# Row tiles at other distances from the weights, a two-tile copy, 128-row broadcasts and a wide norm in a float32r network kernel

## The chip, the cores and the metric

One core of a Trainium2 chip runs the whole program in one launch. The metric is the device time of an execution in microseconds (us), lower is better; the kernel before was timed three times. All instruction times come from one profiled execution of that kernel. The engines are PE (TensorE matmul), DVE (VectorE), ACT (ScalarE), POOL (GpSimd) and SP (SyncE, which issues the weight DMAs).

## The reference, cut

256 tokens of width 1024 go through one recurrent block, two hybrid attention layers and a last norm, all in float32.

```python
def first_block(x, ...):                     # DEPTH 1
    hn = rmsnorm(h, norm1_w)
    gates, z, xbc, dt_raw, lru_x, lru_y = split(hn @ w_in)
    ...                                      # Mamba-2 mixer, RG-LRU mixer, gated sum
    h = h + merged @ w_out
    hn = rmsnorm(h, norm2_w)
    g, u = split(hn @ w_ffn_in)              # 2816 wide each
    h = h + (silu(g) * u) @ w_ffn_out
    return rmsnorm(h, norm_f_w)

def hybrid_layer(x, ...):                    # twice
    proj = rms_norm(x, attn_norm_w) @ w_in
    ...                                      # retention, sparse and dilated attention
    x = x + mixed @ w_out
    h = rms_norm(x, mlp_norm_w)
    return x + square(relu(h @ w_up)) @ w_down   # 4096 wide
```

## The kernel before, in words

Activations lie with the feature on the partition and the 256 tokens (`T`) along the row, as row tiles of 128 features by 256 tokens. Every large product is made of float32r matmuls in three parts: `mm3` (L330 to L333) multiplies the high part of the weight with the high part of the row tile, the high with the low, and the low with the high. In `run_a` (L335) a 128x128 block of the weight is loaded and a 128x256 row tile streams past it; in `run_b` (L361) a block of the row tile is loaded and up to 512 columns of the weight stream. A unit is a 512-column strip of a weight matrix; it is cut into pieces of 128x1024 elements, 24 matmuls in `run_a`. The weights come over SP's queue as 1 MB chunks into three `raw` buffers. ACT makes the high part of a piece (`hi`, L254), DVE the low (`lo`, L255), into rings of five; `next_piece` splits four pieces ahead of use. The order of units is a list (`PLAN`); small work (scans, attention, transposes) is inserted between matmuls by generators, moved on by `tick` after each pair of column blocks (counts in `TICKS` and `YIELDS`).

The stages in order of time are: `in` (input projection with both mixers between), `wo`, the FFN's input (`fg`, `fu`, tiles `xnh`/`xnl`, 44 pieces) and output (`fo`, tiles `ah`/`al`), then per layer `l` the mixer's projections (`mix`, `run_a` and `run_b`), its output (`mx` tiles), the MLP's `up` (`xnh`/`xnl`, 32 pieces) and `down` (`dn`, tiles `mah`/`mal`; layer 0 as `run_a`, layer 1 as `run_b`).

`pair_tiles` (L407) allocates the high and low tiles of a stage with some padding and starts the data at an element offset from the table `OFF`; everything else is allocated in steps of 512 bytes. With the address of the moving tile less that of the loaded weight, modulo 512 bytes, as the **distance**, each stage therefore has one distance, the same for all its row tiles, `hi` and `lo` alike.

`Norm` (L886) collects the squares of the residual: `add` accumulates them into a 128x2x256 tile `sqa` (L910), `bank_done` also makes the row tiles and, at the last one, a small square root `pre` (L923) that brings ACT's table. The row tiles are not scaled by the norm; the scale `rb` multiplies the matmul's result when the PSUM banks are evacuated. `hook` runs `sums` after a given piece of the first unit and `spread` after another (marks `FM`, `QM`, `UM`): `sums` (L946) reduces `sqa` over the partitions by fp32 matmuls with a column of ones (two passes each), eight passes per accumulator; `rsqrt_act` or `rsqrt_cols` work on 128x2; `spread` (L481, L484) turns the two columns into a 128x256 tile `rb` with two transposes and a copy by ACT.

`bc` (L668) belongs to the Mamba mixer. For two heads it broadcasts a row of cumulative sums `csp` over all partitions with a pair of matmuls (L674) whose weight is a column of `idr` repeated 128 times, on 64 rows: rows 0 to 31 the high part, 32 to 63 the low. The pairs stand between the matmuls of a `run_a`, some of them directly behind the L693 matmuls of another small task.

Of the kernel before, what the change touches and what calls it, by code (L numbers as in the profile page):

```python
# [17 lines left out]
T = 256  # L18
# [11 lines left out]
def _pv_layout():  # L30
    at = 0
    for name, n in (("norm1", 8), ("bgate", 16), ("scw", 96), ("scb", 24), ("snw", 16), ("lcw", 40),
# [22 lines left out]
OFF = {"in": (48, 64), "ffn": (64, 80), "mix0": (16, 32), "up0": (48, 64), "mix1": (32, 48), "up1": (48, 64),  # L55
       "ah": (0, 0), "mx": (8, 8), "mah0": (120, 120), "mah1": (16, 16)}
# [67 lines left out]
def _build(ctx, tc, nc, A, out):  # L124
# [192 lines left out]
    def tpb():  # L317
        return bank("tp", 1)
# [88 lines left out]
    def pair_tiles(pool, k, stage, names, tags=(None, None), pads=(128, 128)):  # L407

        ab = []
        for n, t, pad, o in zip(names, tags, pads, OFF[stage]):  # L410
            kw = dict(tag=t) if t else {}
            tl = pool.tile([128, k * T + pad], F32R, name=n, **kw)
            ab.append(tl[:, o:o + k * T].rearrange("p (k t) -> p k t", t=T))
        return ab

    def xn_tiles():
        xn_n[0] += 1
        stage = STAGES[xn_s[0]]
        xn_s[0] += 1
        return pair_tiles(cp, 8, stage, (f"xnh{xn_n[0]}", f"xnl{xn_n[0]}"), ("xnh", "xnl"), (112, 104))  # L420

# [39 lines left out]
    def rsqrt_act(src, scale, bias, tag, pool=None):  # L461

        rs_n[0] += 1
        n = src.shape[1]
        v, t = (sm.tile([128, n], F32, tag=tag + k, name=f"{k}{tag}{rs_n[0]}") for k in "vt")
        y = (pool or sm).tile([128, n], F32, tag=tag + "y", name=f"y{tag}{rs_n[0]}")
        S.activation(y, src, AF.Sqrt, scale=scale, bias=bias)
        V.tensor_scalar(v, src, scale, bias, op0=OP.mult, op1=OP.add)
        V.reciprocal(y, y)
        for i in range(n):  # L470
            c = slice(i, i + 1)
            V.scalar_tensor_tensor(t[:, c], y[:, c], y[:, c], v[:, c], op0=OP.mult, op1=OP.mult)
        V.tensor_scalar(t, t, -0.5, 1.5, op0=OP.mult, op1=OP.add)
        V.tensor_mul(y, y, t)
        return y
# [20 lines left out]
    with ExitStack() as st0:  # L496
# [50 lines left out]
        idr = cp.tile([64, 32], F32R, name="idr")  # L547
        V.tensor_add(idr, ident[0:64, 0:32], ident[0:64, 32:64])
# [32 lines left out]
    csp = p1.tile([64, T], F32R, name="csp")  # L581
# [5 lines left out]
    def dt_task(bdt):  # L587
# [26 lines left out]
        S.activation(csp, csf, AF.Copy)  # L614
# [31 lines left out]
    def ssm_task(g, xsf):  # L646
# [21 lines left out]
        def bc(j):  # L668
            ps = scb()
            M = p1.tile([128, 2, 384], F32, tag="M", bufs=2, name=f"M{g}{j}")  # L670
            for i in range(2):
                hh = 8 * g + 2 * j + i
                o = ps[:, i * 256:i * 256 + 256]
                PE.matmul(o, idr[:, hh:hh + 1].to_broadcast([64, 128]), csp, start=(i == 0), stop=True,  # L674
# [211 lines left out]
    class Norm:  # L886


        def __init__(self, wcol, second=None, sq=None, act=False):
# [47 lines left out]
        def sums(self):  # L937
# [3 lines left out]
            self.r1t = None  # L941
            ps = tpb()
            for a in range(n):
                for b in range(2):
                    for i in range(2):
                        PE.matmul(ps[:, 2 * a + b:2 * a + b + 1], self.acc[a][:, i, b * 128:b * 128 + 128], ones[:, 0:1],  # L946
                                  start=(i == 0), stop=(i == 1))
# [13 lines left out]
        def spread(self):  # L961
            self.rb = spread(self.rt, npl[0], "rb")
# [8 lines left out]
    nrm = Norm(lambda t: pvc("norm2", t), sq=(p1, "cv"), act=True)  # L971
# [11 lines left out]
    with ExitStack() as st:  # L983
        pf = st.enter_context(tc.tile_pool(name="pf", bufs=1, side="right", reuse_waits="tile"))
        ah, al = pair_tiles(pf, 22, "ah", ("ah", "al"))
        X = opnd(nrm.xn)
        for i, (a, b) in enumerate(FT):
            bg = run_a(f"fg{i}", X, hook=nrm.hook(FM) if i == 0 else None)
# [24 lines left out]
    def mixers(l, nrm):  # L1013
# [273 lines left out]
        nrm2 = Norm(lambda t: pvc("mlp", 8 * l + t), act=True)  # L1287
# [10 lines left out]
    def mlp(l, nrm):  # L1298
        with ExitStack() as st:
            pf = st.enter_context(tc.tile_pool(name=f"pf{l}", bufs=1, side="right", reuse_waits="tile"))  # L1300
            ah, al = pair_tiles(pf, 32, f"mah{l}", (f"mah{l}", f"mal{l}"))
            X = opnd(nrm.xn)
            last = l == 1
# [14 lines left out]
            for i in range(8):  # L1318
                bu = run_a(f"up{i}_{l}", X, hook=nrm.hook(UM) if i == 0 else None)
# [19 lines left out]
            for n in range(2):  # L1339
# [4 lines left out]
                for b in range(2):  # L1344
                    parts = ((0, 0, 512), (1, 0, 512)) if n == 0 else ((0, 0, 512), (1, 0, 256), (2, 256, 256))
                    parts = parts[b:1 + b * len(parts)]
                    for i, (k, c0, w) in enumerate(parts):
# [7 lines left out]
                        q = pf.tile([128, 512], F32, tag="fq", bufs=2, name=f"fq{n}{b}{i}")  # L1355
# [50 lines left out]
```

## Time and profile before

| | |
|---|---|
| median of 3 runs | 1198.53 us (1198.38 to 1199.04) |
| the profiled execution | 1198.39 us |
| its span, first to last instruction | 1196.6 us |
| PE busy | 1183.8 us (99%), 9369 instructions |
| PE weight loads (PEld), beside PE | 1115.4 us (93%) |
| DVE busy | 844.9 us (71%) |
| ACT busy | 700.4 us (59%) |
| mean granted TensorE clock | 0.999 |
| DMA | 205.21 MB, mean 171 GB/s |

Busy time is the union of an engine's records. A matmul's record is longer than the time to the next one's start, so the busy share does not tell how closely the matmuls follow; the number of them in a stretch does.

### The profile page before, as it was taken

Reading aid. Unit: us, or ns where it says so; the run is one execution under the profiler, and the core shown is the slowest. Engines: PE = TensorE matmul, PEld = TensorE weight load, DVE = VectorE, ACT = ScalarE, POOL = GpSimd, SP = SyncE. Lnnn points to the kernel's source line nnn. Section 1 sums busy time; section 2 is a strip of 40 time slices with the busy share of each in tenths; the row PEclk is TensorE's granted clock in tenths of the full one; section 3 lists DMA queues with packets and bytes.
Section 4 is the critical chain, followed back from the end, with each engine's and each line's share of the span. In section 5 each row is a group of like instructions: output and inputs, shape, how many; then the busy total and the mean of one; then the engine's idle time right before and its main releaser. Section 6 shows DMA issues by size and latency. Waiting matters only on the chain.

```text
span 1196.6 us, 22653 instructions
## 1 busy us (share of the span) xinstructions
PE 1183.8 (99%) x9369; PEld 1115.4 (93%) x9369; DVE 844.9 (71%) x1483; ACT 700.4 (59%) x1071; POOL 4.6 (0%) x12
## 2 busy tenths in 40 slices
PE   8999999999999999999999999999999999999997
PEld 8998999999999999999887799999997969999886
DVE  7888988987676766656977586755469576667453
ACT  7698888767465444454445565544345376655342
POOL 0000000000000000000000000000000000000000
PEclk9999999999999999999999999999999999999999
DMA  8455545656555555555453356565554435565550
GB/s 293 149 179 175 160 139 159 203 177 206 192 188 175 178 179 189 179 169 194 142 171 106 124 177 196 192 204 185 177 168 128 155 93 172 177 194 194 196 191 36
DMA packets 109382, 205.21 MB, mean 171 GB/s; under 512 B 5792, under 2 KB 15776, under 8 KB 109152
## 3 DMA queue, kind: packets, MB, share of 16 engines
q1 hardware_dynamic: 108560, 201.09, 51.6%
q0 software_dynamic: 576, 2.62, 0.6%
q8 instruction: 73, 1.20, 0.4%
q14 instruction: 29, 0.24, 0.1%
q10 hardware_dynamic: 144, 0.07, 0.0%
HBM read 202.71 MB, written 1.05 MB: 170 GB/s over the span
## 4 chain that ended last, share of the span: by engine, by line
PE 88%; DVE 6%; ACT 4%; issue 1%; DMA 0%; SPq 0%; ACTq 0%; DVEq 0%
PE ps_mm L331 24%; PE ps_mm L333 23%; PE ps_mm L332 23%; PE ps_mm L381 3%; PE ps_mm L383 3%; PE ps_mm L382 3%; PE ps_sc L328 2%; DVE lo L255 2%; PE ps_o L1127 1%; PE ps_o L693 1%; ACT hi L254 1%; DVE acc L1073 1%; PE ps_tp L1114 1%; DVE m L1072 1%; PE ps_sc L674 1%
## 5 line engine op out<-in xcount | busy, mean ns | idle before, releaser
L255 DVE TENSOR_TENSOR lo<-raw,hi 128x1024 fp32r<-128x1024 f32 (+2 forms) x382 | 461.9, 1213 | 272.4 <-ACT hi L254 268.9
L254 ACT ACTIVATE hi<-raw 128x1024 fp32r<-128x1024 f32 (+2 forms) x382 | 400.8, 1054 | 408.7 <-PE ps_mm L332 315.8
L331 PE MATMUL ps_mm<-xnh,hi 128*128 128x256 f32 x1736 | 487.9, 281 | 0.0
L332 PE MATMUL ps_mm<-xnl,hi 128*128 128x256 f32 x1736 | 486.0, 280 | 0.2 <-DVE xnl L492 0.2
L333 PE MATMUL ps_mm<-xnh,lo 128*128 128x256 f32 (+1 forms) x1736 | 484.9, 279 | 0.0
L331 PEld LDWEIGHTS ps_mm<-xnh,hi 128*128 128x128 f32 x1736 | 326.8, 188 | 3.8 <-issue 2.5
L332 PEld LDWEIGHTS ps_mm<-xnl,hi 128*128 128x128 f32 x1736 | 327.5, 189 | 1.6 <-DVE xnl L492 0.4
L333 PEld LDWEIGHTS ps_mm<-xnh,lo 128*128 128x128 f32 (+1 forms) x1736 | 326.8, 188 | 0.6 <-DVE lo L255 0.2
L333 PE MATMUL ps_mm<-mah,lo 128*128 128x256 f32 x256 | 70.7, 276 | 0.0
L331 PE MATMUL ps_mm<-mah,hi 128*128 128x256 f32 x256 | 70.7, 276 | 0.0
L332 PE MATMUL ps_mm<-mal,hi 128*128 128x256 f32 x256 | 70.7, 276 | 0.0
L382 PE MATMUL ps_mm<-lo,mah 128*128 128x256 f32 (+1 forms) x160 | 55.6, 348 | 0.0
L381 PE MATMUL ps_mm<-hi,mah 128*128 128x256 f32 (+1 forms) x160 | 55.6, 347 | 0.0
L383 PE MATMUL ps_mm<-hi,mal 128*128 128x256 f32 (+1 forms) x160 | 55.5, 347 | 0.0
L331 PE MATMUL ps_mm<-ah,hi 128*128 128x256 f32 x176 | 48.6, 276 | 0.0
L333 PE MATMUL ps_mm<-ah,lo 128*128 128x256 f32 x176 | 48.6, 276 | 0.0
L332 PE MATMUL ps_mm<-al,hi 128*128 128x256 f32 x176 | 48.6, 276 | 0.0
L331 PEld LDWEIGHTS ps_mm<-mah,hi 128*128 128x128 f32 x256 | 48.0, 188 | 0.0
L332 PEld LDWEIGHTS ps_mm<-mal,hi 128*128 128x128 f32 x256 | 48.0, 188 | 0.0
L333 PEld LDWEIGHTS ps_mm<-mah,lo 128*128 128x128 f32 x256 | 48.0, 188 | 0.0
L381 PE MATMUL ps_mm<-hi,xnh 128*128 128x512 f32 x96 | 39.2, 408 | 0.0
L383 PE MATMUL ps_mm<-hi,xnl 128*128 128x512 f32 x96 | 38.0, 396 | 0.0
(384 smaller groups left out, 1885.3 us busy)
## 6 DMA issues: line engine op xcount, KB each, us to landing
raw<-in_w_in SPq DMA_DIRECT2D x61, 1024.0 KB, 5.0
raw<-in_w_up SPq DMA_DIRECT2D x32, 1024.0 KB, 5.3
raw<-in_w_down SPq DMA_DIRECT2D x32, 1024.0 KB, 4.9
raw<-in_w_ffn_in SPq DMA_DIRECT2D x22, 1024.0 KB, 5.0
raw<-in_w_ffn_out SPq DMA_DIRECT2D x10, 1024.0 KB, 4.9
raw<-in_w_out_ssm SPq DMA_DIRECT2D x8, 1024.0 KB, 5.0
raw<-in_w_out SPq DMA_DIRECT2D x16, 512.0 KB, 3.8
raw<-in_w_out_lru SPq DMA_DIRECT2D x4, 1024.0 KB, 4.9
```

Source lines behind the costliest of these rows:

```text
L254: S.activation(hi, raw, AF.Copy)
L255: V.tensor_sub(lo, raw, hi.bitcast(F32))
L328: PE.matmul(o, w, x_, start=True, stop=True)
L331: PE.matmul(ps, wh, xh, start=start, stop=False, skip_group_check=True)
L332: PE.matmul(ps, wh, xl, start=False, stop=False, skip_group_check=True)
L333: PE.matmul(ps, wl, xh, start=False, stop=stop, skip_group_check=True)
L381: PE.matmul(o, xh[:, ts], hi[:, k, cs], start=st, stop=False, skip_group_check=True)
L382: PE.matmul(o, xh[:, ts], lo[:, k, cs], start=False, stop=False, skip_group_check=True)
L383: PE.matmul(o, xl[:, ts], hi[:, k, cs], start=False, stop=sp, skip_group_check=True)
L674: PE.matmul(o, idr[:, hh:hh + 1].to_broadcast([64, 128]), csp, start=(i == 0), stop=True, skip_group_check=True)
L693: PE.matmul(ps[64 * i:64 * i + 64, c], xtok[g][:, b, (2 * j + i) * 64:(2 * j + i) * 64 + 64], M[:, i, m], start=(j % 2 == 0 and b == 0), s ...
L1072: V.max(m8, acc[:, a:b])
```

## The change

- The offsets of `OFF` are set so that all row tiles of the norms and the `mx` tiles stand at one distance. `other_place` copies the row tiles 6 and 7 (high by ACT, low by DVE) to a buffer at another distance; one piece of the FFN's first unit, of the first `up` unit of layer 0, and of the first and the third `up` unit of layer 1 reads the copy: always the last piece of the unit, 24 matmuls.

| stage | distance before | distance after |
|---|---|---|
| in, wo, fo, up of both layers, dn of layer 0 | 192 | 192 |
| FFN input | 256 | 192 |
| mix of layer 0: run_a / run_b | 64 / 448 | 192 / 320 |
| mix of layer 1: run_a / run_b | 128 / 384 | 192 / 320 |
| mx of both layers | 320 | 192 |
| the pieces that read a copy | | 256 |
| dn of layer 1 (run_b) | 256 | 256 |

- The pairs of `bc` use 128 rows: `idr` has the two further diagonals of `ident` and rows 64 to 127 of `csp` are set to zero by one DVE operation.
- `sums` first adds the two halves of `sqa` on DVE, so that half as many one-column matmuls remain.
- The norms of the FFN and of both MLPs are `full`: one fp32 matmul of a 128x128 tile of ones with the folded 128x256 squares gives the sum on every partition, `rsqrt_full` works on 128x256, and `spread` does nothing.

```diff
@@ -52,8 +52,9 @@
-OFF = {"in": (48, 64), "ffn": (64, 80), "mix0": (16, 32), "up0": (48, 64), "mix1": (32, 48), "up1": (48, 64),
-       "ah": (0, 0), "mx": (8, 8), "mah0": (120, 120), "mah1": (16, 16)}
+OFF = {"in": (48, 64), "ffn": (48, 64), "mix0": (48, 64), "up0": (48, 64), "mix1": (48, 64), "up1": (48, 64),
+       "ah": (0, 0), "mx": (104, 104), "mah0": (120, 120), "mah1": (16, 16),
+       "altffn": (16, 16), "altup0": (8, 8), "altup1": (16, 16)}
@@ -404,11 +405,13 @@
-    def pair_tiles(pool, k, stage, names, tags=(None, None), pads=(128, 128)):
+    def pair_tiles(pool, k, stage, names, tags=(None, None), pads=(128, 128), bufs=None):
...
             kw = dict(tag=t) if t else {}
+            if bufs:
+                kw["bufs"] = bufs
@@ -418,6 +421,13 @@
         return pair_tiles(cp, 8, stage, (f"xnh{xn_n[0]}", f"xnl{xn_n[0]}"), ("xnh", "xnl"), (112, 104))
+    def other_place(pool, pair, stage):
+        alt = pair_tiles(pool, 2, "alt" + stage, (f"alh{xn_n[0]}", f"all{xn_n[0]}"), ("fq", "fq"), bufs=2)
+        S.activation(alt[0], pair[0][:, 6:8, :], AF.Copy)
+        V.tensor_copy(alt[1], pair[1][:, 6:8, :])
+        return lambda k: (alt[0][:, k - 6, :], alt[1][:, k - 6, :]) if k >= 6 else (pair[0][:, k, :], pair[1][:, k, :])
@@ -470,6 +480,20 @@
+    def rsqrt_full(src, scale, bias, work, pool, tag):
+        rs_n[0] += 1
+        v, t = work[:, 0, :], work[:, 1, :]
+        y = pool.tile([128, T], F32, tag=tag, name=f"{tag}{rs_n[0]}")
+        S.activation(y, src, AF.Sqrt, scale=scale, bias=bias)
+        V.tensor_scalar(v, src, scale, bias, op0=OP.mult, op1=OP.add)
+        V.reciprocal(y, y)
+        V.tensor_mul(t, y, y)
+        V.tensor_mul(t, t, v)
+        V.tensor_scalar(t, t, -0.5, 1.5, op0=OP.mult, op1=OP.add)
+        V.tensor_mul(y, y, t)
+        return y
@@ -544,8 +568,9 @@
             S.activation(h[:, f:f + 2, :].rearrange("p a b -> p (a b)"), hb[f // 2], AF.Copy)
-        idr = cp.tile([64, 32], F32R, name="idr")
-        V.tensor_add(idr, ident[0:64, 0:32], ident[0:64, 32:64])
+        idr = cp.tile([128, 32], F32R, name="idr")
+        V.tensor_add(idr, ident[:, 0:32], ident[:, 32:64])
@@ -578,7 +603,7 @@
     cst = p1.tile([128, 3, 32], F32, name="cst")
-    csp = p1.tile([64, T], F32R, name="csp")
+    csp = p1.tile([128, T], F32R, name="csp")
@@ -611,7 +636,8 @@
         csf = cs[:, 0:2, :].rearrange("p a b -> p (a b)")
-        S.activation(csp, csf, AF.Copy)
+        V.tensor_scalar(csp[64:128, :], tri[64:128, 0:T], 0.0, None, op0=OP.mult)
+        S.activation(csp[0:64, :], csf, AF.Copy)
@@ -671,7 +697,7 @@
                 o = ps[:, i * 256:i * 256 + 256]
-                PE.matmul(o, idr[:, hh:hh + 1].to_broadcast([64, 128]), csp, start=(i == 0), stop=True,
+                PE.matmul(o, idr[:, hh:hh + 1].to_broadcast([128, 128]), csp, start=(i == 0), stop=True,
@@ -886,7 +912,8 @@
-        def __init__(self, wcol, second=None, sq=None, act=False):
+        def __init__(self, wcol, second=None, sq=None, act=False, full=False):
+            self.full = full
@@ -939,12 +966,19 @@
             self.r1t = None
+            for a in range(n):
+                V.tensor_add(self.acc[a][:, 0, :], self.acc[a][:, 0, :], self.acc[a][:, 1, :])
             ps = tpb()
+            if self.full:
+                PE.matmul(ps[:, 0:T], ones, self.acc[0][:, 0, :], start=True, stop=True)
+                work = npl[0].tile([128, 2, T], F32, tag="sq", bufs=2, name=f"rw{self.n}")
+                self.rb = rsqrt_full(ps[:, 0:T], 1.0 / D, epsc, work, npl[0], "rb")
+                return
...
                 for b in range(2):
-                    for i in range(2):
-                        PE.matmul(ps[:, 2 * a + b:2 * a + b + 1], self.acc[a][:, i, b * 128:b * 128 + 128], ones[:, 0:1],
-                                  start=(i == 0), stop=(i == 1))
+                    PE.matmul(ps[:, 2 * a + b:2 * a + b + 1], self.acc[a][:, 0, b * 128:b * 128 + 128], ones[:, 0:1],
+                              start=True, stop=True)
@@ -959,6 +993,8 @@
         def spread(self):
+            if self.full:
+                return
@@ -968,7 +1004,7 @@
     npl = [None]
-    nrm = Norm(lambda t: pvc("norm2", t), sq=(p1, "cv"), act=True)
+    nrm = Norm(lambda t: pvc("norm2", t), sq=(p1, "cv"), act=True, full=True)
@@ -984,8 +1020,9 @@
         X = opnd(nrm.xn)
+        X2 = other_place(pf, nrm.xn, "ffn")
         for i, (a, b) in enumerate(FT):
-            bg = run_a(f"fg{i}", X, hook=nrm.hook(FM) if i == 0 else None)
+            bg = run_a(f"fg{i}", X2 if i == 0 else X, hook=nrm.hook(FM) if i == 0 else None)
@@ -1284,7 +1321,7 @@
         ob_ = [[mmb() for _ in range(2)] for _ in range(2)]
-        nrm2 = Norm(lambda t: pvc("mlp", 8 * l + t), act=True)
+        nrm2 = Norm(lambda t: pvc("mlp", 8 * l + t), act=True, full=True)
@@ -1300,6 +1337,7 @@
             X = opnd(nrm.xn)
+            X2 = other_place(pf, nrm.xn, f"up{l}")
@@ -1316,7 +1354,7 @@
             for i in range(8):
-                bu = run_a(f"up{i}_{l}", X, hook=nrm.hook(UM) if i == 0 else None)
+                bu = run_a(f"up{i}_{l}", X2 if i in (0, 2 * l) else X, hook=nrm.hook(UM) if i == 0 else None)
@@ -1352,7 +1390,7 @@
                         V.tensor_add(d, d, banks[k][:, 0:w])
-                        q = pf.tile([128, 512], F32, tag="fq", bufs=2, name=f"fq{n}{b}{i}")
+                        q = pf.tile([128, 2 * T + 128], F32, tag="fq", bufs=2, name=f"fq{n}{b}{i}")
```

How this moves instructions, at three places. Names are tiles, with a buffer's number behind; "x4" is so many alike in a row (an fp32 instruction there is two passes on PE). Line numbers after the change are those of the changed file.

PE at the FFN norm's sums, after the third piece of `fg0`, before (`sqa` is the accumulator of squares):

```order
L332 MATMUL ps_mm_4624<-xnl_4342,hi_4535 128x256
L333 MATMUL ps_mm_4624<-xnh_4341,lo_4536 128x256
L946 MATMUL ps_tp_4711<-ones,sqa_2_4340 128x1 x4
L331 MATMUL ps_mm_4623<-xnh_4341,hi_4563 128x256
L332 MATMUL ps_mm_4623<-xnl_4342,hi_4563 128x256
L333 MATMUL ps_mm_4623<-xnh_4341,lo_4564 128x256
L331 MATMUL ps_mm_4623<-xnh_4341,hi_4563 128x256
```

PE at the same place, after the change:

```order
L333 MATMUL ps_mm_4629<-xnl_4343,hi_4536 128x256
L334 MATMUL ps_mm_4629<-xnh_4342,lo_4537 128x256
L974 MATMUL ps_tp_4717<-sqa_2_4341,ones 128x256
L332 MATMUL ps_mm_4628<-alh_4624,hi_4564 128x256
L333 MATMUL ps_mm_4628<-all_4625,hi_4564 128x256
L334 MATMUL ps_mm_4628<-alh_4624,lo_4565 128x256
L332 MATMUL ps_mm_4628<-alh_4624,hi_4564 128x256
```

The eight passes (four instructions of two) give way to one instruction of two passes, and the piece behind it reads the copy `alh`/`all`. Before, PE also has this three matmuls into the next unit, which has nothing in its place after:

```order
L332 MATMUL ps_mm_4767<-xnl_4342,hi_4625 128x256
L333 MATMUL ps_mm_4767<-xnh_4341,lo_4626 128x256
L481 MATMUL ps_tp_4756<-ct,yna_4718 128x128 x2
L331 MATMUL ps_mm_4767<-xnh_4341,hi_4625 128x256
L332 MATMUL ps_mm_4767<-xnl_4342,hi_4625 128x256
```

The transposes of `spread` are gone there and, alike, in both MLPs.

DVE around the same norm, before (`lo` is a weight split, `vna`, `yna`, `tna` the small square root, `fsg` the evacuation of the unit's banks):

```order
L910 TENSOR_TENSOR sqa_2_4340<-sqa_2_4340,sq_135_14_4608 128x512
L1003 TENSOR_TENSOR wfa<-pv 128x8
L1005 COPY wfac<-wfa 128x8
L255 TENSOR_TENSOR lo_4684<-raw_4509,hi_4683 128x1024
L255 TENSOR_TENSOR lo_4727<-raw_4509,hi_4726 128x1024
L468 TENSOR_SCALAR vna_4716<-ps_tp_4711,epsc 128x2
L469 RECIPROCAL yna_4718<-yna_4718 128x2
L472 SCALAR_TENSOR_TENSOR tna_4717<-yna_4718,vna_4716 128x1 x2
L473 TENSOR_SCALAR tna_4717<-tna_4717 128x2
L474 TENSOR_TENSOR yna_4718<-yna_4718,tna_4717 128x2
L255 TENSOR_TENSOR lo_4770<-raw_4567,hi_4769 128x1024
L992 TENSOR_TENSOR fsg_4761<-ps_mm_4623,rb_4759 128x512
```

DVE at the same place, after the change:

```order
L937 TENSOR_TENSOR sqa_2_4341<-sqa_2_4341,sq_135_14_4609 128x512
L970 TENSOR_TENSOR sqa_2_4341<-sqa_2_4341 128x256
L429 COPY all_4625<-xnl_4343 128x512
L256 TENSOR_TENSOR lo_4689<-raw_4510,hi_4688 128x1024
L1040 TENSOR_TENSOR wfa<-pv 128x8
L1042 COPY wfac<-wfa 128x8
L256 TENSOR_TENSOR lo_4729<-raw_4510,hi_4728 128x1024
L493 TENSOR_SCALAR rw_4719<-ps_tp_4717,epsc 128x256
L494 RECIPROCAL rb_4720<-rb_4720 128x256
L256 TENSOR_TENSOR lo_4767<-raw_4568,hi_4766 128x1024
L495 TENSOR_TENSOR rw_4719<-rb_4720 128x256
L496 TENSOR_TENSOR rw_4719<-rw_4719 128x256
```

The fold L970 and the copy L429 stand between the last add of squares and the next split, and the square root's operations are 128x256 wide, with a split among them, ahead of the evacuation.

PE at the sums of the first mixer's norm, which stays narrow and has two accumulators, before:

```order
L333 MATMUL ps_mm_6769<-xnh_6035,lo_6616 128x256
L946 MATMUL ps_tp_6798<-ones,sqa_4_6033 128x1 x4
L331 MATMUL ps_mm_6768<-xnh_6035,hi_6643 128x256
L332 MATMUL ps_mm_6768<-xnl_6036,hi_6643 128x256
L333 MATMUL ps_mm_6768<-xnh_6035,lo_6644 128x256
L331 MATMUL ps_mm_6768<-xnh_6035,hi_6643 128x256
L946 MATMUL ps_tp_6798<-ones,sqa_4_6034 128x1 x4
L332 MATMUL ps_mm_6768<-xnl_6036,hi_6643 128x256
```

PE at the same sums, after the change:

```order
L333 MATMUL ps_mm_6766<-xnl_6033,hi_6640 128x256
L980 MATMUL ps_tp_6797<-ones,sqa_4_6030 128x1 x2
L334 MATMUL ps_mm_6766<-xnh_6032,lo_6641 128x256
L332 MATMUL ps_mm_6766<-xnh_6032,hi_6640 128x256
L333 MATMUL ps_mm_6766<-xnl_6033,hi_6640 128x256
L980 MATMUL ps_tp_6797<-ones,sqa_4_6031 128x1 x2
L334 MATMUL ps_mm_6766<-xnh_6032,lo_6641 128x256
L332 MATMUL ps_mm_6766<-xnh_6032,hi_6640 128x256
```

Each group has two instructions in place of four, and the first stands 13 rows later in PE's order.

## Rows read from the trace of the kernel before

**Rows 1.** The page: busy time, share, instructions; shares of the chain that ended last.
```profile
PE 1183.8 (99%) x9369; PEld 1115.4 (93%) x9369; DVE 844.9 (71%) x1483; ACT 700.4 (59%) x1071; POOL 4.6 (0%) x12
...
PE 88%; DVE 6%; ACT 4%; issue 1%; DMA 0%; SPq 0%; ACTq 0%; DVEq 0%
```

**Rows 2.** Windows of PE: us, busy, busy (count), granted clock, DMA share, GB/s.
```profile
302.00:342.00 40.00, 40.00 (x342) 1.00 0.55 185
...
380.00:492.00 112.00, 112.00 (x936) 1.00 0.56 184
495.00:552.00 57.00, 57.00 (x506) 1.00 0.56 185
618.00:634.00 16.00, 16.00 (x144) 1.00 0.36 117
679.00:693.00 14.00, 14.00 (x122) 1.00 0.60 205
708.00:781.00 73.00, 73.00 (x646) 1.00 0.60 193
783.00:868.00 85.00, 85.00 (x753) 1.00 0.57 187
934.00:950.00 16.00, 16.00 (x137) 1.00 0.33 110
...
1036.00:1100.00 64.00, 64.00 (x567) 1.00 0.61 198
```

**Rows 3.** Timeline of PE at two transposes: start us, duration us, instruction, count.
```profile
300.33 0.38 PE L481 MATMUL ps_tp<-ct,yn 128*128 128x128 f32 x2
...
706.43 0.38 PE L481 MATMUL ps_tp<-ct,yna 128*128 128x128 f32 x2
```

**Rows 4.** Timeline of PE at two `bc` pairs; L674's group: busy us, mean ns.
```profile
97.85 0.28 PE L333 MATMUL ps_mm<-xnh,lo 128*128 128x256 f32 x1
98.05 0.50 PE L674 MATMUL ps_sc<-csp,idr 64*128 64x256 f32 x2
98.48 0.39 PE L331 MATMUL ps_mm<-xnh,hi 128*128 128x256 f32 x1
98.71 0.28 PE L332 MATMUL ps_mm<-xnl,hi 128*128 128x256 f32 x1
...
106.36 0.50 PE L674 MATMUL ps_sc<-csp,idr 64*128 64x256 f32 x2
106.79 0.38 PE L331 MATMUL ps_mm<-xnh,hi 128*128 128x256 f32 x1
107.01 0.28 PE L332 MATMUL ps_mm<-xnl,hi 128*128 128x256 f32 x1
...
L674 PE MATMUL ps_sc<-csp,idr 64*128 64x256 f32 x32 | 8.0, 329 | 0.0
```

**Rows 5.** Timeline of PE at the FFN norm's sums and transposes.
```profile
374.21 0.95 PE L946 MATMUL ps_tp<-ones,sqa 128*128 128x1 f32 x8
...
375.21 0.28 PE L332 MATMUL ps_mm<-xnl,hi 128*128 128x256 f32 x1
...
378.32 0.38 PE L481 MATMUL ps_tp<-ct,yna 128*128 128x128 f32 x2
...
378.66 0.28 PE L332 MATMUL ps_mm<-xnl,hi 128*128 128x256 f32 x1
```

**Rows 6.** Timeline of PE at a two-pass fp32 matmul 128x256.
```profile
130.36 0.60 PE L655 MATMUL ps_sc<-bcT 128*128 128x256 f32 x2
...
130.91 0.28 PE L332 MATMUL ps_mm<-xnl,hi 128*128 128x256 f32 x1
```

**Rows 7.** Timeline of DVE: the FFN norm's last add of squares.
```profile
371.90 0.69 DVE L910 TENSOR_TENSOR sqa<-sqa,sq 128x512 f32<-128x512 f32 x1 [0.29 <-ACT pre L923]
```

**Rows 8.** The page's groups: a 512-wide matmul of `run_b`.
```profile
L381 PE MATMUL ps_mm<-hi,xnh 128*128 128x512 f32 x96 | 39.2, 408 | 0.0
```

**Rows 9.** Waits of PE: us in total, times, longest us.
```profile
PE ps_tp L481 <- DVE ync L446: 0.8, 2, 0.5
```

## The prediction

> **What bounds the kernel now.** I read the page first: PE is busy 1183.8 of 1196.6 us and carries 88% of the chain that ended last, DVE is busy 71% of the span [rows 1]. So the time is the number of matmuls times the interval between their starts, plus the places where PE is held up. The busy time cannot tell intervals apart, because records overlap, so I then read the windows of PE over stretches that hold only 128x256 float32r matmuls [rows 2]. The count of a window takes in about two that lie across its edges. The reader is to see three paces at one granted clock, 1.00: 112/934 = 119.9 ns in the FFN's input stage, where weights and row tiles lie 256 bytes apart; 57/504 = 113.1 and 73/644 = 113.4 ns in its output stage and in the first MLP's up stage (192 apart); and 40/340 = 117.6 ns at the end of the input stage, also 192 apart. At 192 there are thus two paces, and the timeline shows that an interruption may set either: the two transposes at 300.33 are followed by 117.6 ns up to the end of that stage, the two at 706.43 by 113.4 ns through two stages [rows 2, 3]. I call them fast (113.3) and slow (117.8); one costs 4.5 ns per matmul against the other. At 64 bytes I find 16/142 = 112.7, at 320 14/120 = 116.7, at 128 16/135 = 118.5 ns. Supply does not bind: dn0 runs at 113.2 ns with a DMA share of 0.57, the FFN at 119.9 with 0.56 [rows 2].
>
> The sum is made against the profiled execution, 1198.39 us (span 1196.6 and 1.8 around it); the median of the runs, 1198.53, is 0.14 above it.
>
> **The change, part by part.**
>
> *FFN input, 256 to 192.* 1056 matmuls (44 pieces of 24). The first 72 come before the copy and go on in the slow pace of the stages ahead, as from 302 to 342 [rows 2]: 72 x 2.1 ns = -0.15. The next 24 read the copy at 256 and cost what they cost now. The other 960 go from 119.9 to 113.3 or to 117.8: -6.3 or -2.0. I take fast, -6.3, since the one place where the program steps from 256 to 192 now, the FFN's end, is followed by the fast pace from 495 on [rows 2]. With that the output stage needs no step any more and stays fast, 0.
>
> *The broadcasts of `bc`.* 16 pairs on 64 rows (x32) become 128 rows. A pair alone: from the L333 at 97.85 to the L332 at 98.71 pass 0.86 us for four matmuls, of which the pace asks 4 x 0.113 = 0.45 [rows 4]. The pair itself starts 0.20 late, takes 0.43 and the matmul behind it 0.23. If full rows bring the pair to the pace, it saves 0.40; nine cases are like that. In seven the pair stands behind the L693 matmuls: from 106.36 to 107.01 0.65 us for three that need 0.34 or, with the switch that remains behind L693, 0.45: 0.20. Together 9 x 0.40 + 7 x 0.20 = -5.0. Bounds: 0 (the delay is not the rows') and 16 x 0.40 = -6.4. I take -5.0: every full-row float32r matmul of the windows runs without such a gap. The zero rows cost DVE one 64x256 operation, once, early, beside 71% busy.
>
> *`full` for three norms.* The eight one-column passes take from 374.21 to the second matmul behind them at 375.21, 1.00 us, less 0.12 of a regular one, 0.88 lost; the two transposes 378.32 to 378.66, 0.34 less 0.12, 0.22 [rows 5]. The new fp32 128x256 matmul has its like at L655: 130.36 to 130.91, 0.55, less 0.12, 0.43 [rows 6]. Each norm saves 0.67, three 2.0. Bounds: 0 and 3 x 1.10 = -3.3. The six wide DVE operations of `rsqrt_full` (at most 0.69 each, the 128x512 add's time [rows 7]) come to some 4 us in the FFN, hidden: only the evacuation of the banks reads their result, after the piece that follows; without that cover the four PSUM banks would hold PE.
>
> *Sums folded by DVE.* Passes halve where the sums stay narrow: 16 to 8 and 8 to 4, 12 x 0.88/8 = -1.3 [rows 5]. The added add sits between the last square and PE's sums. In the FFN the last add ends 371.90 + 0.69 = 372.59, PE comes at 374.21: 1.6 us of room [rows 5, 7]. In the MLPs the room is less; each could wait up to 0.69.
>
> *Other distances.* mix1's run_a, 432 matmuls, 128 to 192: 118.5 to 113.3 or 117.8, -2.2 or -0.3; I take -1.2. The mix output, 384 matmuls, 320 to 192: 0 or 384 x 3.4 ns = -1.3; -0.8. mix0's run_a, 64 to 192: pace 112.7 now, 0 (or +1.3 for the 287 that could change pace). The 288 512-wide matmuls of run_b [rows 8], whose distance goes from 448 and 384 to 320: no row at 320, both present ones agree, 0 (+-1.7, 6 ns each, the spread of the paces).
>
> *Copies.* 72 matmuls of the MLPs go from 113.3 to 119.9: +0.5. ACT and DVE each copy 128x512 three times, under 0.7 us, ahead of the piece that reads them, behind the last row tile; ACT's `pre` moves up in exchange, and a split, four pieces ahead of use, moves back.
>
> *Waits.* PE waits 0.8 us for `ync` in the mixers [rows 9], set by DVE; what PE wins just ahead is lost there. With the later add: +0.5 (0 to 2.9 = 0.8 + 3 x 0.69).
>
> Sum: -0.15 - 6.3 - 5.0 - 2.0 - 1.3 - 1.2 - 0.8 + 0.5 + 0.5 = -15.75: **1182.6 us**.
>
> [...] The FFN shows 119.9 ns at 256 bytes and the output stage 113.1 at 192, same shape, clock and supply [rows 2]. [...] Chance 0.05.
>
> **Rivals.** *The copy does not set the fast pace.* At 192 the FFN runs slow, -2.0 in place of -6.3: **1186.9**. For it: one step from 256 to 192 is a single case, and both paces occur at 192. Chance 0.18.
>
> *Full rows bring nothing to `bc`.* Some other thing (the broadcast weight, the change of bank) makes the gap: +5.0, **1187.6**. Chance 0.08.
>
> *The slow pace everywhere (the other side).* After `full` no transposes stand in the first MLP, where at 706.43 they were followed by the fast pace [rows 3]; the copy stands in their place. If a step from 256 to 192 leaves the slow pace, it is kept to the next interruption, and fo, up0, dn0 and up1, whose fast matmuls I count as 524, 687, 767 and 718 (rows 2 show 504, 644, 751 and 565 of them), lose 2696 x 4.5 ns = 12.1. With the FFN at -2.0 and the other distances at 0 the sum is -15.75 + 4.3 + 2.0 + 12.1 = +2.65: **1201.0**. Without these 2696 the sum would stand at -9.45; it is slower by over 2.4 us once 11.85/0.0045 = 2633 of them turn slow, and within 2.4 us from 7.05/0.0045 = 1567 on. Against it: the one step seen. Chance 0.06, of which 0.03 inside 0.2%.
>
> **How the numbers follow.** Forecast 0.63, rivals 0.18, 0.08, 0.05, 0.06. Likeliest: 1182.6. Below it lie the slow stretches of input stage and w_out (1068 and 192 matmuls, 5.7 us at 4.5 ns), which other interruptions may turn fast: low end 1177. The high end takes in both 1187s and the rule's 1190.6: 1191. About 0.2% (2.4 us) is what a measurement can tell from no change: faster 0.94, within 0.03, slower 0.03.
>
> **What would show it.** In the changed profile: FFN stretch with 990 rather than 936 matmuls in 112 us; `bc` pairs 0.11 apart; one two-pass L974 in place of eight passes and no transposes in FFN and MLPs; fo, up0, dn0, up1 still near 113 ns. Wrong if the FFN shows 117.8, if the stage behind a copy does, or if PE waits for DVE grow by over 1 us.

## The result, and the profile after

The changed kernel takes **1183.67 us** (median of four runs, 1183.2 to 1184.76), the kernel before 1198.55 beside it (four runs, 1198.38 to 1199.04): a ratio of 0.9876, 95% interval 0.9859 to 0.9894. The forecast was 1182.6, in a range of 1177 to 1191. The profiled execution took 1183.59 us, its span is 1181.8.

The page of the changed kernel, the lines that answer to [rows 1]:

```profile
PE 1168.6 (99%) x9333; PEld 1103.4 (93%) x9333; DVE 854.7 (72%) x1493; ACT 702.3 (59%) x1071; POOL 4.6 (0%) x12
...
PE 88%; DVE 6%; ACT 4%; issue 1%; DMA 0%; SPq 0%; ACTq 0%; DVEq 0%
```

PE's busy time falls by 15.2 us, the span by 14.8. DVE has 9.8 us more work and ACT 1.9, and little of it shows (0.6 us of a wait, below): the chain is the same mix as before. So all of the gain is PE's own, in how closely its matmuls follow and in how many passes it makes. The windows say where (PE; us, busy, count, granted clock, DMA share, GB/s), over the stretches that answer to [rows 2]:

```profile
299.00:338.00 39.00, 39.00 (x333) 1.00 0.57 189
...
376.00:481.00 105.00, 105.00 (x929) 1.00 0.62 195
484.00:541.00 57.00, 57.00 (x505) 1.00 0.56 186
607.00:623.00 16.00, 16.00 (x139) 1.00 0.30 100
667.50:681.00 13.50, 13.50 (x120) 1.00 0.64 218
697.00:769.00 72.00, 72.00 (x638) 1.00 0.62 202
771.00:856.00 85.00, 85.00 (x753) 1.00 0.57 187
922.00:937.00 15.00, 15.00 (x135) 1.00 0.30 87
...
1033.00:1085.00 52.00, 52.00 (x462) 1.00 0.61 200
```

The FFN now has 927 matmuls in 105 us, 113.3 ns each, where it had 119.9. Its output, the first MLP and the second are where they were. The second mixer's stretch (922) goes from 118.5 to 15/133 = 112.8, the mix output (667.5) from 116.7 to 114.4. The end of the input stage (299) is still slow, 39/331 = 117.8, and the first mixer's stretch (607) has become slow, 16/137 = 116.8. In windows this short the edges count for an ns or more: from start to start of the matmuls the trace gives 113.3 for the second mixer and the mix output now (118.7 and 117.8 before), and for the first mixer 117.8 now and 113.3 before. The clock is 1.00 in all of them.

Stage by stage, from the first matmul of a stage to the first of the next in the two traces (us):

| stage | before | after | difference | forecast |
|---|---|---|---|---|
| in | 341.9 | 338.4 | -3.5 | -5.0 |
| wo | 22.6 | 22.6 | 0 | 0 |
| FFN input | 127.8 | 120.6 | -7.2 | -7.1 |
| FFN output | 59.9 | 59.8 | 0 | 0 |
| mix, layer 0 | 140.7 | 139.9 | -0.8 | -1.0 |
| up, layer 0 | 88.6 | 88.1 | -0.5 | -0.5 |
| down, layer 0 | 87.0 | 87.0 | 0 | 0 |
| mix, layer 1 | 141.0 | 138.4 | -2.5 | -1.8 |
| up, layer 1 | 90.5 | 90.1 | -0.3 | -0.4 |
| down, layer 1 | 88.5 | 88.5 | 0 | 0 |

The forecast's column shares its terms out over the stages (a norm's 0.67 with its stage, the mixer sums as 0.9 and 0.4, the mix output half and half, the waits with the mixers). In the timeline of PE, a lone broadcast pair and one behind the L719 matmuls (L693 before) now read:

```profile
97.68 0.28 PE L334 MATMUL ps_mm<-xnh,lo 128*128 128x256 f32 x1
97.79 0.40 PE L700 MATMUL ps_sc<-csp,idr 128*128 128x256 f32 x2
...
98.14 0.28 PE L333 MATMUL ps_mm<-xnl,hi 128*128 128x256 f32 x1
```

```profile
105.78 0.50 PE L700 MATMUL ps_sc<-csp,idr 128*128 128x256 f32 x2
106.12 0.28 PE L332 MATMUL ps_mm<-xnh,hi 128*128 128x256 f32 x1
106.24 0.28 PE L333 MATMUL ps_mm<-xnl,hi 128*128 128x256 f32 x1
```

Four matmuls take 98.14 - 97.68 = 0.46 us where they took 0.86, and the other case 106.24 - 105.78 = 0.46 where it took 0.65 [rows 4]. But the pairs now do something else: they turn the pace over. Behind the last pair of the first group (one behind L719 matmuls) nothing interrupts the matmuls for 150 and more. A window of PE there in the kernel before:

```profile
201.00:217.00 16.00, 16.00 (x144) 1.00 0.63 199
```

and in the changed kernel:

```profile
199.00:215.00 16.00, 16.00 (x138) 1.00 0.62 198
```

16/142 = 112.7 against 16/136 = 117.6 ns, fast before and slow after. The FFN's sums, which answer to [rows 5]:

```profile
370.54 0.59 PE L974 MATMUL ps_tp<-sqa,ones 128*128 128x256 f32 x2
370.78 0.47 PE L332 MATMUL ps_mm<-alh,hi 128*128 128x256 f32 x1
371.09 0.28 PE L333 MATMUL ps_mm<-all,hi 128*128 128x256 f32 x1
371.20 0.28 PE L334 MATMUL ps_mm<-alh,lo 128*128 128x256 f32 x1
```

From 370.54 to the second matmul behind, at 371.09, 0.55 us: what [rows 6] show of the two-pass matmul at another place, and no transposes behind it.

The wait of PE that grew most is the one for `ync`, where [rows 9] had 0.8 (us in total, times, longest):

```profile
PE ps_tp L505 <- DVE ync L456: 1.4, 2, 0.8
```

### The profile page after: what moved, and what is told of

It is laid out like the page before. It is cut to its first block, busy times and chain, and to the rows that moved or that the text cites. A ratio compares the mean times of both kernels' runs of the same rounds, so it can differ in the third digit from the quotient of the medians.

```text
span 1181.8 us, 22586 instructions
## 1 busy us (share of the span) xinstructions
PE 1168.6 (99%) x9333; PEld 1103.4 (93%) x9333; DVE 854.7 (72%) x1493; ACT 702.3 (59%) x1071; POOL 4.6 (0%) x12
## 4 chain that ended last, share of the span: by engine, by line
PE 88%; DVE 6%; ACT 4%; issue 1%; DMA 0%; SPq 0%; ACTq 0%; DVEq 0%
PE ps_mm L332 23%; PE ps_mm L333 23%; PE ps_mm L334 23%; PE ps_mm L382 3%; PE ps_mm L384 3%; PE ps_mm L383 3%; PE ps_sc L329 2%; DVE lo L256 2%; PE ps_o L1164 1%; PE ps_o L719 1%; ACT hi L255 1%; DVE acc L1110 1%; PE ps_tp L1151 1%; DVE m L1109 1%; DMA raw<-in_w_in 0%
## 5 line engine op out<-in xcount | busy, mean ns | idle before, releaser
L332 PE MATMUL ps_mm<-xnh,hi 128*128 128x256 f32 x1704 | 475.3, 279 | 0.0
L333 PE MATMUL ps_mm<-xnl,hi 128*128 128x256 f32 x1704 | 474.7, 279 | 0.2 <-DVE xnl L516 0.2
L334 PE MATMUL ps_mm<-xnh,lo 128*128 128x256 f32 (+1 forms) x1704 | 473.8, 278 | 0.0
L332 PEld LDWEIGHTS ps_mm<-xnh,hi 128*128 128x128 f32 x1704 | 319.5, 188 | 3.1 <-issue 2.5
L333 PEld LDWEIGHTS ps_mm<-xnl,hi 128*128 128x128 f32 x1704 | 320.1, 188 | 1.8 <-DVE xnl L516 0.4
L334 PEld LDWEIGHTS ps_mm<-xnh,lo 128*128 128x128 f32 (+1 forms) x1704 | 319.6, 188 | 0.6 <-DVE lo L256 0.2
```

Of the source, the lines that this page charges most:

```text
L332: PE.matmul(ps, wh, xh, start=start, stop=False, skip_group_check=True)
L333: PE.matmul(ps, wh, xl, start=False, stop=False, skip_group_check=True)
L334: PE.matmul(ps, wl, xh, start=False, stop=stop, skip_group_check=True)
```

## The experiments

Theory: PE's pace between 128x256 float32r matmuls depends on the distance (120 at 256; at 192 it can be 113.3 or 117.8), any break in the stream (other small matmuls or a wait between two matmuls of a product) can set it anew, and a step from 256 to 192 sets the fast one. Rivals: the stage or the two-pass sum sets it; another buffer is enough; the row count of the broadcasts does nothing.

**1. No copies** (the changed kernel).

```diff
-        X2 = other_place(pf, nrm.xn, "ffn")
-            bg = run_a(f"fg{i}", X2 if i == 0 else X, ...)
+            bg = run_a(f"fg{i}", X, ...)
...
```

> The changed kernel without the copies: every piece reads the row tiles at distance 192. Theory (the step from 256 back to 192 sets the fast pace in the FFN): 960 FFN matmuls stay at 117.8 ns, the FFN stage takes about 124.8 us in place of 120.6, and the whole 1183.6 + 4.3 - 0.5 (three copy pieces at 113.3 or 117.8 in the MLPs) = 1187.4 us; if the MLPs too fall to the slow pace, up to 6.5 (layer 0, 1436 matmuls) and 2.5 us (layer 1, 558) more, 1196. Rival (the distance alone, or the break by the two-pass sum, sets the pace): the FFN stays at 113.3 ns, 1183.1 us.

Measured 1184.74 and 1185.75 us. The theory missed here: the FFN took 120.45 us, fast from behind the two-pass sum on (376 to 481: 105/926 = 113.4 ns), 0.15 less than with the copy piece. So in this execution the break alone had left the fast pace. The MLPs' up stages cost 0.27 us more each for another reason: PE waits there for the fold, which it does not in the changed kernel (waits of PE). That the missing copies move `pre` and the splits, and so the fold, is likely but not shown:

```profile
PE ps_tp L974 <- DVE sqa L970: 0.9, 2, 0.5
```

The input stage, which the edit does not touch, took another 0.8 us.

**2. Copies at distance 192.**

```diff
-       "altffn": (16, 16), "altup0": (8, 8), "altup1": (16, 16)}
+       "altffn": (0, 0), "altup0": (120, 120), "altup1": (0, 0)}
```

> The changed kernel with all copies kept, but placed so that they too lie at distance 192. Theory (the step in distance sets the pace, not the change to another buffer and not the copying): as without copies, FFN stage about 124.8 us, 1187.4 us or more. Rival (another buffer is enough): FFN at 113.3 ns behind the copy, 1183.1 us.

Measured 1183.42 and 1184.1 us, the FFN 120.45 us: again fast without any step. By runs 1 and 2 alone the copies looked like ballast; run 10 repeats this kernel.

**3. The distances alone** (the kernel before).

```diff
-OFF = {... "ffn": (64, 80), "mix0": (16, 32), ... "mix1": (32, 48), ... "mx": (8, 8), ...}
+OFF = {... "ffn": (48, 64), "mix0": (48, 64), ... "mix1": (48, 64), ... "mx": (104, 104), ...}
```

> The kernel before with the distances of the change alone (FFN, mixes, mx to 192; no copies, narrow sums, 64 rows). Theory: the FFN loses the 120 ns and takes one of the two paces of 192, slow unless its norm's transposes turn it: 1198.4 - 2.2 (FFN slow) - 2.2 (mix of layer 1 and mx, fast) = 1194.0 us, or 1189.5 if the transposes turn it fast. Rival (the distance does not set the pace, the stage does): FFN stays at 119.9 ns and the whole at 1198.4 us.

Measured 1189.5 and 1190.12 us: the FFN 121.2 in place of 127.8, the second mixer 138.8 in place of 141.0. Eight offsets in a table bring 9 of the 15 us. Some 4 of these are the FFN's fast pace, which this execution had from its one-column sums at 374.5 on (the transposes at 378.5 found it fast already); the offsets alone do not secure it. The rival, that the stage and not the distance sets 119.9 ns, falls: at 192 the same stage had 100/883 = 113.3 ns (385 to 485).

**4. Broadcasts on 64 rows** (the changed kernel).

```diff
-        idr = cp.tile([128, 32], F32R, name="idr")
+        idr = cp.tile([64, 32], F32R, name="idr")
...
-                PE.matmul(o, idr[:, hh:hh + 1].to_broadcast([128, 128]), csp, ...)
+                PE.matmul(o, idr[:, hh:hh + 1].to_broadcast([64, 128]), csp, ...)
```

> The changed kernel with the broadcast pairs back on 64 rows. Theory (the rows make the delay): a lone pair again costs 0.40 us, one behind the other small matmuls 0.20: input stage 338.4 + 5.0 us, the whole 1188.6 us, apart from up to 1.4 us that a different mix of fast and slow stretches in that stage gives or takes (before: 1364 fast and 1068 slow, after: 1095 and 1383). Rival (the rows do nothing): within 1.4 us of 1183.6 us.

Measured 1188.31 (profiled) and 1185.96 us. The input stage took 343.1 us, 4.7 more, with 83 slow matmuls fewer (1300 against 1383, 0.4 us): 64 rows cost 5.1 us in gaps. The term is right. The second run, 2.4 lower, has no trace.

The rows also change the pace. From the first pair to 5 us behind the last of each of the two groups, 173 intervals are slow (117 to 119 ns from start to start) in run 4 and 475 in the changed kernel, 1.3 us. In the three profiles with 64 rows (the kernel before, runs 3 and 4) the pace behind a pair is fast in 44 of 45 clear cases; in the eleven with 128 rows it is the other one than ahead of the pair in 143 of 162. The same window of PE in run 4, to be held against the 138 of the changed kernel:

```profile
202.00:218.00 16.00, 16.00 (x144) 1.00 0.59 198
```

The 83 hide this, since run 4 has some 275 slow matmuls more ahead of the first pair, where the two programs do the same. So full rows are worth about 5.1 - 1.3 = 3.8 us here, not 5.1.

**5. A step in the gates** (the changed kernel, one more copy).

```diff
     def do_gate(i):
-        gates(i, run_a(f"gt{i}", X))
+        Xg = X
+        if i == 2:
+            kh, kl = [p1.tile([128, 4, T], F32R, tag=t, ...)[:, 16:528] ... for t in ("lTh", "lTl")]
+            S.activation(kh, xn[0][:, 6:8, :], AF.Copy)
+            V.tensor_copy(kl, xn[1][:, 6:8, :])
+            Xg = lambda k: (kh[:, k - 6, :], kl[:, k - 6, :]) if k >= 6 else (xn[0][:, k, :], xn[1][:, k, :])
+        gates(i, run_a(f"gt{i}", Xg))
```

> The changed kernel with one more copy: the last piece of the gate unit gt2 (24 matmuls, in the input stage) reads a copy of row tiles 6 and 7 at distance 256. In all five profiles so far the two transposes at about 297 us leave 622 matmuls in the slow pace, up to the FFN norm's sums. Theory (a step from 256 back to 192 sets the fast pace): the w_out stage takes 21.8 in place of 22.6 us, some 550 matmuls gain 4.5 ns each, less 0.05 to 0.15 for the copy piece: 1183.7 - 2.3 = 1181.4 us. Rival (only a gap in PE's stream can change the pace, a step in distance cannot): w_out stays at 22.6 us, 1183.8 us.

**6. The same copy at distance 192** (offset 0 in place of 16).

> The same extra copy in gt2, but at distance 192. Theory (the step in distance acts): no effect, w_out 22.6 us, 1183.7 us. Rival (a change to another buffer is enough): w_out 21.8 us, 1181.3 us.

Run 5 measured 1181.22 us (1181.05 to 1182.45, four runs), run 6 1183.23 and 1183.25. The windows of PE in the units behind the copy and in `wo`, of run 5:

```profile
307.00:337.00 30.00, 30.00 (x267) 1.00 0.60 201
340.00:360.00 20.00, 20.00 (x179) 1.00 0.60 206
```

and of run 6:

```profile
307.00:337.00 30.00, 30.00 (x257) 1.00 0.57 191
341.00:361.00 20.00, 20.00 (x172) 1.00 0.59 198
```

30/265 = 113.2 against 30/255 = 117.6 ns, by nothing but 64 bytes in the place of the copy. This is the clean test of the step, since the slow pace stands there in every profile: in all 14 the four one-column sums at 292 to 297 turn fast into slow, and the two transposes 4 us behind them find it slow and leave it slow. The timeline of PE in run 5 shows the step itself, with the end of the copy piece in the first rows:

```profile
305.78 0.28 PE L334 MATMUL ps_mm<-kicklTl,hi 128*128 128x256 f32 x1
305.90 0.28 PE L335 MATMUL ps_mm<-kicklTh,lo 128*128 128x256 f32 x1
306.02 0.28 PE L333 MATMUL ps_mm<-sTh,hi 128*128 128x256 f32 x1
...
306.37 0.28 PE L333 MATMUL ps_mm<-sTh,hi 128*128 128x256 f32 x1
306.49 0.28 PE L334 MATMUL ps_mm<-sTl,hi 128*128 128x256 f32 x1
306.60 0.28 PE L335 MATMUL ps_mm<-sTh,lo 128*128 128x256 f32 x1
306.72 0.28 PE L333 MATMUL ps_mm<-sTh,hi 128*128 128x256 f32 x1
```

The intervals are 0.12 up to the step, then four irregular ones (to 306.49), then 0.113 or 0.114 for 547 matmuls, as the count of the windows shows.

**7. The last stage at 192** (the weights move there).

```diff
-       "mah1": (16, 16)
+       "mah1": (32, 32)
```

> The changed kernel with the last stage's row tiles (layer 1's down product, the weights moving) shifted from distance 256 to 192. Theory (256 costs the moving weights as it costs moving row tiles): the 178 matmuls of 256 columns go from 119.9 to 113.3 ns, -1.2 us, and the 288 of 512 columns gain nothing to 6 ns each, up to -1.7 us: stage 88.5 to 86 or 87 us, the whole 1181 to 1182.5 us. Rival (with the weights moving the distance does nothing, as 448 and 384 in the mixers were alike): 1183.7 us.

Measured 1184.79 us (1184.64 to 1185.68). Both expectations missed: the stage took 89.6 us, 1.1 more. From start to start the 128x512 matmuls took 233.0 ns in place of 227.9, while the 128x256 ones took 117.8 in place of 119.5. Their group in the page's form (line, operation, busy us, mean ns of one), of the changed kernel:

```profile
L382 PE MATMUL ps_mm<-hi,mah 128*128 128x512 f32 x96 | 37.5, 391 | 0.0
```

and of run 7:

```profile
L382 PE MATMUL ps_mm<-hi,mah 128*128 128x512 f32 x96 | 37.9, 395 | 0.0
```

So with 512-wide moving weights 256 is the better of the two; the order of the distances is not the same for the two shapes.

**8. Narrow norms** (the changed kernel with copies and fold, `full` off).

```diff
-    nrm = Norm(..., sq=(p1, "cv"), act=True, full=True)
+    nrm = Norm(..., sq=(p1, "cv"), act=True)
...
-        nrm2 = Norm(..., act=True, full=True)
+        nrm2 = Norm(..., act=True)
```

> The changed kernel with the three norms narrow again (one-column sums after the fold, transposes back). Theory: each norm has four passes fewer than the kernel before thanks to the fold (0.44 us) and costs about 0.23 us more than the wide one: 1183.7 + 0.7 = 1184.4 us, if the pace of the stages behind stays. Rival (the two-pass sum is what puts the stages behind in the fast pace): FFN and output stage slow, up to +6.7 us, 1190 us.

Measured 1191.84 and 1192.38 us. Windows of PE in the FFN's input and output stages of run 8:

```profile
378.00:485.00 107.00, 107.00 (x911) 1.00 0.55 184
490.00:548.00 58.00, 58.00 (x495) 1.00 0.51 176
```

107/909 = 117.7 and 58/493 = 117.6: both slow, 6.8 us together. The timeline of PE shows where (`xnh` behind `alh` is the step):

```profile
374.02 0.28 PE L334 MATMUL ps_mm<-alh,lo 128*128 128x256 f32 x1
374.14 0.29 PE L332 MATMUL ps_mm<-xnh,hi 128*128 128x256 f32 x1
374.26 0.28 PE L333 MATMUL ps_mm<-xnl,hi 128*128 128x256 f32 x1
374.38 0.28 PE L334 MATMUL ps_mm<-xnh,lo 128*128 128x256 f32 x1
374.50 0.38 PE L505 MATMUL ps_tp<-ct,yna 128*128 128x128 f32 x2
374.64 0.36 PE L332 MATMUL ps_mm<-xnh,hi 128*128 128x256 f32 x1
374.84 0.28 PE L333 MATMUL ps_mm<-xnl,hi 128*128 128x256 f32 x1
```

The transposes of `spread` come three matmuls behind the step and set the pace anew, here to slow. In the first MLP of the same execution they left the fast one (707 to 777: 70/618 = 113.3 ns). So the wide norm is worth its own passes and, more in these two runs, the break that it no longer makes behind the copy.

**9. A step of three matmuls.** As run 5, but `Xg` gives the copy for the last of its 32 calls alone.

> As the run with the step in the gates (which took 1181.2 us: w_out 21.76 us, 547 fast matmuls behind the step), but only the last three matmuls of gt2 read the copy at distance 256, not 24. Theory (the step itself turns the pace, not a stretch at 256): w_out again 21.8 us, some 570 fast matmuls, 1181.1 us. Rival (a longer stretch at 256 is needed): w_out 22.6 us and 1183.6 us.

Measured 1182.13 us (1181.17 to 1182.47): `wo` 21.76 us, 548 fast matmuls behind the step. Three do as well as 24.

**10. Run 2's kernel again**, six runs.

> The changed kernel with its copies at distance 192 again, in more runs: the FFN's pace then hangs on what the two-pass sum leaves. Theory (a break at the same place leaves the same pace in each execution): all runs within 1.5 us of 1183.6 us. Rival (the pace behind a break is a matter of chance, and the step is what makes it certain): some runs 2.4 us (FFN output alone) to 6.7 us (FFN and its output, 1485 x 4.5 ns) above the others.

Measured 1190.21, 1190.02, 1190.88, 1182.95, 1189.76 and 1189.62 us. The kernel before, beside it, took 1198.51 to 1199.91 in six runs and 1205.16 to 1206.36 in five. The profiled one is of the higher kind. Windows of PE in up and down of layer 0, in run 10 (1190.21 us):

```profile
697.00:769.00 72.00, 72.00 (x614) 1.00 0.59 191
776.00:862.00 86.00, 86.00 (x732) 1.00 0.54 181
```

and of the same kernel in run 2 (1183.42 us):

```profile
697.00:769.00 72.00, 72.00 (x638) 1.00 0.63 203
772.00:856.00 84.00, 84.00 (x743) 1.00 0.57 189
```

72/612 and 86/730, 117.6 and 117.8 ns, against 72/636 and 84/741, 113.2 and 113.4. The program is the same to the byte. Behind the two-pass sum of the first MLP PE stays in one pace for 1462 matmuls, 6.5 us. So the rival holds: **the pace behind a break is not a property of the program**, it differs between executions of one kernel. (Run 2 ran on another chip than run 10, but run 10's own six runs, five high and one at 1182.95, were on one.)

The two traces do not part at that sum, though. They differ from the input stage on, at the first mixer's stretch too (607 to 624: fast in run 2, slow in run 10), and they come to the sum in different paces: run 2 slow, with the sum 0.12 us after the matmul ahead of it, and leaves fast; run 10 fast, with the sum 0.30 us after, and leaves slow. So "chance" may only mean that the pace behind hangs on the pace ahead or on the length of the break, and both of these rivals were left untested. The traces have a case against each alone: in run 1 PE came fast, waited 0.43 us and left fast; in run 11 it came to the same sum slow, with no wait as in run 2, and left slow. What decides it stays open.

**11. Steps of three everywhere** (run 9, and in `other_place` the copy only for the last of 32 calls).

> The run with three matmuls at 256 in the gates, with the copy pieces of the FFN and the MLPs cut to their last three matmuls as well. Theory (three are enough everywhere): four times 21 matmuls at 113.3 in place of 119.9 ns, -0.55 us against the run before it (1181.2 at its best): 1180.6 us at best, all runs within 1.5 us of it. Rival (three are not enough behind the two-pass sum): up0 and dn0 or FFN and fo slow in some runs, +6.5 us.

**12. The changed kernel again**, five runs.

> The changed kernel itself in more runs, beside more of the kernel before. Theory (the step from 256 to 192 makes the fast pace certain behind the sums of FFN and MLPs): all runs within 1.6 us of 1183.2 us, while the kernel before and the kernel with its copies at 192 show runs 6 to 7 us above their best. Rival (the changed kernel has them too, the first four runs were lucky): some runs near 1190 us.

**Runs 11 and 12.** On one chip, with eleven runs of the kernel before (three at 1198.55 to 1199.58, eight at 1204.75 to 1207.13): run 11 took 1182.38 us (1180.24 to 1183.13, six runs), run 12 1185.38 (1184.8 to 1185.8, five). Both are up to an us wider or higher than was expected of them (within 1.5 of 1180.6, within 1.6 of 1183.2), but no run of either lies 6 us above its best, and that was the question; nor does any of the 31 runs of kernels that have the steps behind wide sums. Run 12 against the kernel before: 0.9844 (0.982 to 0.9868); run 11: 0.9819 (0.9794 to 0.9844). These ratios are against a mix of both groups of the kernel before; against the median of the lower three, 1198.70, run 12 stands at 1185.38/1198.70 = 0.989, near the 0.9876 of the first measurement. Run 11's median is 3.0 us below run 12's, and it is the version to keep; but run 9, with the step in the gates alone and on the same chip, had 1182.13, so the times show nothing of the 0.55 us that the shorter steps were to bring. In run 12's trace the mix of layer 1 has 204 slow matmuls where the first trace of the same kernel has 44; that alone is 0.7 us.

Run 11's trace holds the case that runs 1 and 2 did not: PE comes to the FFN's two-pass sum in the fast pace and leaves it in the slow one, 19 intervals in 371.17 - 368.93 = 2.24 us or 118 ns, until three matmuls read the copy (timeline of PE):

```profile
368.38 0.59 PE L992 MATMUL ps_tp<-sqa,ones 128*128 128x256 f32 x2
...
368.93 0.28 PE L334 MATMUL ps_mm<-xnl,hi 128*128 128x256 f32 x1
...
371.17 0.28 PE L335 MATMUL ps_mm<-xnh,lo 128*128 128x256 f32 x1
371.29 0.28 PE L333 MATMUL ps_mm<-alh,hi 128*128 128x256 f32 x1
```

A window of PE behind that step:

```profile
375.00:479.00 104.00, 104.00 (x920) 1.00 0.59 193
```

104/918 = 113.3 ns.

## Why the prediction was right

- *Bound and supply.* Right: the DMA share of the FFN went to 0.62 at the fast pace and no wait on a split appeared among PE's longest.
- *FFN, 256 to 192.* Right in size (-7.2 for -7.1 with its norm), and the reason given, a step from 256 leaves the fast pace, held wherever it was looked at: in the traces of both kernels and of runs 4 to 12 there are 29 such steps with no break close behind, and the matmuls after all 29 are fast. What I did not see is that the step was not needed in the executions of runs 1 and 2: the sum before it had left the fast pace too. That the copy is needed in some executions is shown by run 10 for the first MLP and by run 11 for the FFN, where the wide sum left the slow pace and the step ended it. What I read from the breaks was wrong, though: the transposes at 300.33 and 706.43 [rows 3] left the pace that they found. From start to start the trace of the kernel before has 117.8 ns from 296.3 on and 113.3 from 703.8 on, directly behind the one-column sums (L718, L946) 4 us ahead of the transposes. And "two paces" is not special to 192: at 64 and 320 bytes the same trace has the same two, 113.3 and 117.8 (at 320 the fast one in 20 intervals, the slow one in 305), and only 256 (120.0) and 128 (118.7 on average) stand apart.
- *Broadcasts.* Right for the gaps: 0.40 and 0.19 per pair, 5.1 us by run 4. The stage shows only 3.5 because 315 more matmuls in it are slow (1383 against 1068), 1.4 us. Nearly all of them, 303, lie where the pairs are (475 slow intervals against 172): the pairs on full rows turn the pace over, which those on 64 rows did not. I had put the pace of this stage at nothing, and only for the better ("may turn fast"); it went the other way, and by the change itself.
- *`full`.* The size of its own passes was right (up of layer 0: -0.67 for the norm, +0.16 for the copy, -0.45 measured). The bound of 0.69 us for each wide DVE operation was not: the FFN's reciprocal (L494) took 1.74 us, the six together 3.8, and no wait of PE for them shows. Its larger worth was missing: without it the FFN's transposes undid the step, and run 8 is 8.4 us above the change.
- *Other distances.* Right in sign. The mix of layer 1 gained 2.5 for 1.8, as its matmuls took the fast pace and not the mean of the two that I put in; that of layer 0 gained 0.8 for 1.0, with PE waiting 1.4 us for `ync` where it waited 0.8: the waits' term, +0.5, measured +0.6. Its run_a, put at 0 with a bound of +1.3, cost about 0.3, as the stretch at 607 turned slow.
- *The rivals.* The slow pace everywhere did not come, but it was the right thing to fear, and at the wrong kernel: my reasoning took the fast matmuls of up and down of layer 0 for something the kernel has, that it can only lose. Their 1431 fast matmuls are one outcome of the kernel before, not its property. In 36 runs of it beside these studies 14 took 1204.75 us or more, some 6 to 8 above the rest, about the price of 1431 matmuls at 4.5 ns (6.4). 13 of the 14 came from one of the chips, out of 22 runs on it, so the chip may have a part in it. No trace of such a run of the kernel before was taken, so that these were up and down of layer 0 is argued from run 10. Against those runs the change is worth about 20 us.
- *The 1190.6 in the range.* That is the sum with the distances worth nothing, -5.0 - 2.0 - 1.3 + 0.5, and 0.05 is its chance. No run shows it; run 3, which moves nothing but addresses, took 1189.5 us profiled against 1198.39, 9 us less, with the FFN at 121.2 in place of 127.8. What the distance acts on inside PE is not shown by any run.

## What to carry to other kernels

Count matmuls per stretch before believing a busy share of 99%: 113, 118 and 120 ns per matmul look the same in it. Where the stationary and the moving tile lie modulo 512 bytes is worth trying as a free parameter (9 us in run 3), for each shape apart (run 7). And when a kernel's runs fall into two groups, look for a stretch whose pace differs between executions (113.2 and 117.6 ns in runs 2 and 10); a few instructions that set it on purpose, with no other break behind them, brought the better group in all 31 runs here. Changing the form of small matmuls in between can cost pace as well as save gaps (run 4: 1.3 us against 5.1), so count the slow matmuls behind them too.

## What had not been expected of the hardware

- The pace of a long stretch of equal matmuls is two-valued (113.3 or 117.8 ns at distance 192, clock 1.00 in both) and is kept for up to 1485 matmuls (the changed kernel, 374 to 542); behind a break it can differ between two executions of one program (run 10 and run 2).
- A pair of float32r matmuls on 128 rows turned the pace over in 143 of 162 clear cases; behind the same pair on 64 rows it was fast in 44 of 45, at 0.2 to 0.4 us of gap per pair (run 4).
- Three matmuls at distance 256 were enough to leave the fast pace at 192: 548 matmuls of it behind them in run 9, 104/918 = 113.3 ns in run 11.
- For 128x512 moving weights 256 is better than 192, 227.9 against 233.0 ns, though for 256 columns 192 is better, 117.8 against 119.5 (run 7).
